# A first difference of weight blocks as a negated ScalarE copy and an accumulating transfer inside SBUF

## The chip, the core and the metric

The kernel runs on one core of a Trainium2 chip. The engines named here are TensorE (PE in the profile; PEld is its weight load), VectorE (DVE), ScalarE (ACT), GpSimd (POOL) and SyncE (SP). Transfers are issued by SP, ACT or POOL and carried by the core's 16 DMA engines. SBUF is the on-chip memory of 128 partitions, PSUM the accumulator memory behind TensorE, in eight banks of 512 float32 per partition. The metric is the device time of one execution in microseconds; all times below are microseconds unless marked ns.

## The reference

One decoder block on 256 tokens of width 2048: a gated convolution and a sparse attention side by side, an output mix, a layer norm, a feed-forward part and a second layer norm. The change is in the feed-forward part:

```python
x = _layer_norm(DN_ALPHA * x + mixed @ w_mix_out[i], ln1_g[i], ln1_b[i])
h = jnp.square(jax.nn.relu(x @ w_mlp_up[i])) @ w_mlp_down[i]
ple = (p[i] @ w_ple[i]) * jax.nn.sigmoid(x @ w_ple_gate[i])
x = _layer_norm(DN_ALPHA * x + h + ple, ln2_g[i], ln2_b[i])
```

`w_mlp_up` is 2048 x 8192, `w_mlp_down` 8192 x 2048, all in float32.

## The kernel before

**Splitting.** Every float32 operand is split in two: ScalarE rounds it to a high part (`hi`, type fp32r), VectorE subtracts that from the original to get the low part (`lo`). A product is then three matmuls: high by high, low by high, high by low. `split` (lines 67 to 70) does this for values and forms, `wchunk` (77 to 89) for a loaded piece of weights: one load to `raw` (four buffers) on SP's queue, `whi` on ScalarE (four buffers, line 86), `wlo` on VectorE (three buffers, line 88), each 128 x 1024 elements.

**The feed-forward loop.** It goes over four blocks `c` of 2048 hidden columns (line 1063). In a block, eight *pairs* `p` compute 256 hidden columns each: `up` (1035) runs `wstat` (91) in four steps of one weight piece, 8 wide matmuls (512 columns, line 106) and 8 narrow ones (256 columns, line 112) per step, then evacuates PSUM to `ab` (1041), adds, applies relu and square (1043 to 1045), splits the result into `h` (1046) and forms sums of its quarter blocks (`sums_to`, 629 to 637). `down` (1051) then multiplies the block's `h` by columns of `w_mlp_down` with `xstat` (131; matmuls at 144, 145, 148).

**Seven products.** The first two of the four column groups of `down` are not computed by `xstat`. For each pair the class `Seven` (639) treats a 2 x 2 arrangement of blocks of `h` and of a 256 x 1024 piece of `w_mlp_down` by seven block products in place of eight. The piece is loaded by `load` (648) as one 1 MB transfer to tile `rs` for even pairs and to the second half of tile `tr` for odd ones. In it `r[:, k, a]` is row block `k`, column half `a`. `b_forms` (653) splits two of its blocks as they are. `t_sums` (657) makes four differences and `t_forms` (664) splits them:

```python
nc.vector.tensor_sub(t13, r[:, :, 512:], r[:, 0, :].rearrange("p (a n) -> p a n", a=2))
nc.vector.tensor_sub(t24[:, 0], r[:, 1, 512:], t13[:, 0])
nc.vector.tensor_sub(t24[:, 1], t24[:, 0], r[:, 1, :512])
```

`t13` and `t24` are the first half of `tr` (two blocks of 512 each) and are used again by every pair. `products` (668) issues the seven products, three matmuls each (line 678), into seven PSUM banks that stay open for the whole block. In blocks 0 to 2 all eight pairs go this way, in block 3 the first four, 28 pieces in all; `second` (681) adds one more column block. Forms of pair `p` are made while pair `p + 1` runs its four steps `i` (`prep`, 1077 and 1090), its products 1 and 3 at step 0 of pair `p + 2`, the other five at step 2 (1085). After the last pair, steps of the third column of `down` take their place (1095 to 1111), and ten sums on the open banks follow (1105). Gates and the output mix use `Seven` too, through `side` (702), with the methods `t_sums` and `t_forms`.

**What sets the order.** The code lists work in program order, and a scheduler that models the engines then fixes one order for each engine, TensorE's interleaving of the blocks above included. On the chip each engine runs its list strictly in that order, and an instruction that waits holds up all behind it on the same engine. `after(x)` keeps an instruction behind `x`. SP's queue carries all weight loads, POOL's a few loads of constants and of the last weights (`rawl`, 1156; `gb_load`, 963).

Of the kernel before, what the change touches and what calls it, by code (L numbers as in the profile page):

```python
# [12 lines left out]
AF = mybir.ActivationFunctionType  # L13
ALU = mybir.AluOpType
# [31 lines left out]
def block_kernel(ctx: ExitStack, tc: tile.TileContext, x, p, w_in, conv_w, cmp_pe_k, cmp_w1_k, cmp_w2_k,  # L46
                 cmp_pe_v, cmp_w1_v, cmp_w2_v, w_conv_out, w_attn_out, w_mix_out, ln1_g, ln1_b,
                 w_mlp_up, w_mlp_down, w_ple, w_ple_gate, ln2_g, ln2_b, rel_bias, onehot, rowmask, out):
    nc = tc.nc
    x, p, w_in, conv_w, w_conv_out, w_attn_out, w_mix_out, w_mlp_up, w_mlp_down, w_ple, w_ple_gate, out = (  # L50
        a[0] for a in (x, p, w_in, conv_w, w_conv_out, w_attn_out, w_mix_out, w_mlp_up, w_mlp_down, w_ple,
                       w_ple_gate, out))
    p = p[0]
# [10 lines left out]
    def after(ins):  # L64
        return tc.issue_after(ins) if ins is not None else nullcontext()

    def split(src, hi, lo):
        last_hi[0] = nc.scalar.activation(hi, src, AF.Copy).ins  # L68
        last_lo[0] = nc.vector.tensor_sub(lo, src, f32(hi)).ins  # L69
        return last_lo[0]  # L70
# [102 lines left out]
    def bank(i):  # L173

        return psum.tile([P, 512], F32, tag=f"b{(2, 3, 0, 1, 4, 5, 6, 7)[i]}", name="s")

    def run(*gens):
        for g in gens:
            for _ in g:
                pass  # L180
# [5 lines left out]
    def weave(main, places, side):  # L186

        done = 0
        for at, _ in enumerate(main):
            while done < len(places) and places[done] <= at:  # L190
                next(side, None)
                done += 1
        run(side)
# [47 lines left out]
    def back(a, first, *dims):  # L241
        return bass.AP(tensor=a.tensor, offset=a.offset + first, ap=[list(a.ap[0])] + [list(d) for d in dims])
# [396 lines left out]
    class Seven:  # L639
# [13 lines left out]
        def b_forms(self, p):  # L653
            b = self.forms[:, self.b(p):self.b(p) + 4]
            split(back(self.raws[p], 0, (1536, 2), (1, 512)), b[:, 0:2], b[:, 2:4])

        def t_sums(self, p):
            r = self.raws[p]
            t13, t24 = self.ts[p] = self.t(p)
# [3 lines that stand above are left out]
# [31 lines left out]
    def in_pairs(w):  # L694
        return w.rearrange("(q k p) n -> p q k n", k=2, p=P)
# [263 lines left out]
    def gb_load(dst, i, v):  # L959

        with after(last_wlo[0]):
            nc.vector.memset(dst[:, i, 0:1], 0.0)
        nc.gpsimd.dma_start(dst[:, i, :], v.to_broadcast([P, D]))
# [71 lines left out]
    def up(c, p, banks):  # L1035

        ps = [b.rearrange("p (a t) -> p a t", a=2) for b in banks]
        yield from wstat(w_mlp_up, c * 2048 + p * 256, x1, None, ps=ps)
        ab = post.tile([P, 2, 2, T], F32, tag="m2", name="ab", bufs=2)
        for f in range(2):  # L1040
            nc.scalar.activation(ab[:, f], ps[f], AF.Copy)  # L1041
        m = ab[:, :, 0, :]
        nc.vector.tensor_add(m, m, ab[:, :, 1, :])
        nc.scalar.activation(m, m, AF.Relu)
        nc.scalar.activation(m, m, AF.Square)
        split(m, h[:, 2 * p:2 * p + 2, 0, :], h[:, 2 * p:2 * p + 2, 1, :])
        if p < sv.n:
            sv.sums[p] = post.tile([P, 4, 2, P], F32R, tag="sg", name="sums")
            sums_to(m, sv.sums[p])

    def down(c, j, banks):
        cs = slice(j * 512, (j + 1) * 512)

        def ev(t, ps):
            nc.vector.tensor_add(y[:, t, cs], y[:, t, cs], ps)
            if c == 3:
                nc.vector.bn_stats(stats2[:, t, j, :], y[:, t, cs])

        k0 = sv.n * 2 % KT if j < 2 else 0
        return xstat(w_mlp_down, j * 512, 512, h, ev, r0=c * 2048 + k0 * P, nkt=KT - k0, ps=banks, kt0=k0), ev  # L1060


    for c in range(4):
        h = big.tile([P, KT, 2, T], F32R, tag="B", name="h")
        forms = post.tile([P, 16, 512], F32R, tag="C", name="forms", bufs=1)
        tr = big.tile([P, 8, 512], F32, tag="O", name="tr")
        tf = tr[:, 0:4]

        def raw(p):
            if p % 2 == 0:  # L1070
                return late.tile([P, 2, 1024], F32, tag="rs", name="rs", bufs=1)
            return tr[:, 4:8].rearrange("p (k a) n -> p k (a n)", k=2)

        sv = Seven(in_pairs(w_mlp_down[c * 2048:(c + 1) * 2048]), 0, h, raw, lambda p: (tf[:, 0:2], tf[:, 2:4]), forms,
                   lambda p: 8 + p % 2 * 4, 0, n=8 if c < 3 else 4)
        acc = sv.acc
        prep = (sv.b_forms, sv.t_sums, sv.t_forms)
        (y00, y01), (y10, y11) = [[y[:, t, a:a + 512] for a in (0, 512)] for t in range(2)]
        u2, u3, u4 = tf[:, 0], tf[:, 1], tf[:, 2]
        if c == 3:  # L1080
            break
        for p in range(8):
            pair = up(c, p, [bank(6), bank(7)] if p == 1 else [bank(0), bank(1)])
            for i in range(4):
                if p >= 2 and i in (0, 2):
                    sv.products(p - 2, (5, 7, 6, 4) if i else (1, 3))
                next(pair)
                if i == 2:
                    sv.load(p)
                if p >= 1 and i < 3:  # L1090
                    prep[i](p - 1)
            run(pair)
        sv.products(6, (1, 3, 5, 7, 6, 4))
        third = down(c, 2, [bank(0), bank(1)])[0]
        for i in range(8):
            next(third)
            if i < 3:
                prep[i](7)
            if i == 3:
                sv.products(7, (1, 3))  # L1100
            if i == 4:
                sv.products(7, (5, 7, 6, 4))
            if i == 5:
                nc.scalar.activation(u2, acc[1], AF.Copy)
                for out_, a, b, op in ((y00, y00, acc[1], ALU.add), (y01, y01, acc[3], ALU.add),
                                       (u2, u2, acc[6], ALU.add), (u4, u2, acc[5], ALU.add),
                                       (u3, u2, acc[7], ALU.add), (y11, y11, acc[5], ALU.add),
                                       (y10, y10, acc[4], ALU.subtract), (y01, y01, u4, ALU.add),
                                       (y10, y10, u3, ALU.add), (y11, y11, u3, ALU.add)):
                    with after(last_wlo[0]):  # L1110
                        nc.vector.tensor_tensor(out_, a, b, op=op)
        run(third)
        ps = bank(4)
        weave(down(c, 3, [bank(2), bank(3)])[0], (1, 3, 5, 6), sv.second(ps))
        nc.vector.tensor_add(y[:, 0, 0:512], y[:, 0, 0:512], ps)
# [3 lines left out]
    for p in range(8):  # L1119
        pair = up(3, p, [bank(6), bank(7)] if p == 1 else [bank(0), bank(1)])  # L1120
        for i in range(4):
            if 2 <= p < 6 and i in (0, 2):
                sv.products(p - 2, (5, 7, 6, 4) if i else (1, 3))
            if p >= 6 and i == 0:
                next(p2)
            next(pair)
            if p < 4 and i == 2:
                sv.load(p)
            if 1 <= p < 5 and i < 3:
                prep[i](p - 1)  # L1130
            if p == 5 and i == 0:
                nc.scalar.activation(u2, acc[1], AF.Copy)
            if p == 5 and i == 3:
                for out_, a, b, op in ((u2, u2, acc[6], ALU.add), (y01, y01, acc[3], ALU.add), (u4, u2, acc[5], ALU.add),
                                       (u3, u2, acc[7], ALU.add), (y11, y11, acc[5], ALU.add),
                                       (y10, y10, acc[4], ALU.subtract), (y01, y01, u4, ALU.add),
                                       (y10, y10, u3, ALU.add), (y11, y11, u3, ALU.add)):
                    with after(last_wlo[0]):
                        nc.vector.tensor_tensor(out_, a, b, op=op)
            if p == 7 and i == 0:  # L1140
                with after(last_wlo[0]):
                    nc.vector.tensor_add(y00, y00, acc[1])
        run(pair)
        if p == 6:
            gb2 = big.tile([P, 2, D], F32, tag="O", name="gb2")
            gb_load(gb2, 0, ln2_g)
# [90 lines left out]
```

## Time and profile before

| what | time |
|---|---|
| median of 3 runs | 1798.98 (1798.4 to 1799.77) |
| span of the profiled execution | 1797.8, which is 1.2 under that median |
| TensorE busy | 1789.0 |
| VectorE busy | 1394.0 |
| ScalarE busy | 1005.9 |
| POOL busy | 18.4 |
| the stage of the four feed-forward blocks | from 1101 on |

The profile is one execution, recorded instruction by instruction. A row of a group tells how many instructions it has, what they wrote and read with shapes, and their durations in ns as minimum, median and maximum, or as busy time and mean. A row of a timeline or of the chain tells start, length, engine, line, operation and count; in square brackets stands how long the engine was idle before and what ended that. A row of waits tells who waited for whom: total, times, longest. A row of transfers tells destination, source, the issuing queue, count, size and the median time from issue to landing. A row of a stretch tells start and end, its length, the busy time and count of PE, PEld, DVE, ACT and POOL, the granted clock, the busy share of the DMA engines and GB/s. Matmuls overlap in the pipeline, so their pace is read from the chain (one after another), not from the length of one.

### The profile page before, as it was taken

Reading aid. Unit: us, or ns where it says so; the run is one execution under the profiler, and the core shown is the slowest. Engines: PE = TensorE matmul, PEld = TensorE weight load, DVE = VectorE, ACT = ScalarE, POOL = GpSimd, SP = SyncE. Lnnn points to the kernel's source line nnn. Section 1 sums busy time; section 2 is a strip of 40 time slices with the busy share of each in tenths; the row PEclk is TensorE's granted clock in tenths of the full one; section 3 lists DMA queues with packets and bytes.
Section 4 is the critical chain, followed back from the end, with each engine's and each line's share of the span. In section 5 each row is a group of like instructions: output and inputs, shape, how many; then the busy total and the mean of one; then the engine's idle time right before and its main releaser. Section 6 shows DMA issues by size and latency. Waiting matters only on the chain.

```text
span 1797.8 us, 24999 instructions
## 1 busy us (share of the span) xinstructions
PE 1789.0 (100%) x9277; PEld 1532.2 (85%) x9277; DVE 1394.0 (78%) x2064; ACT 1005.9 (56%) x1366; POOL 18.4 (1%) x33
## 2 busy tenths in 40 slices
PE   9999999999999999999999999999999999999998
PEld 7889888888888888888888888888888888888886
DVE  6776776777787997897798768886798689768765
ACT  5555555555555555555454745764576376637661
POOL 1000000000000000000000000000000000000010
PEclk9999999999999999999999999999999999999999
DMA  8777665566656665865685577754865586567672
GB/s 260 225 240 202 189 180 165 164 176 177 178 161 187 216 206 188 278 202 181 188 283 167 186 242 239 230 188 160 275 220 165 177 278 208 165 210 233 193 280 71
DMA packets 255849, 365.50 MB, mean 203 GB/s; under 512 B 10821, under 2 KB 175525, under 8 KB 255216
## 3 DMA queue, kind: packets, MB, share of 16 engines
q1 hardware_dynamic: 250944, 352.49, 62.1%
q0 software_dynamic: 2112, 8.81, 1.4%
q10 hardware_dynamic: 2672, 2.62, 0.5%
q8 instruction: 72, 1.18, 0.3%
q14 instruction: 49, 0.40, 0.1%
HBM read 361.76 MB, written 2.12 MB: 202 GB/s over the span
## 4 chain that ended last, share of the span: by engine, by line
PE 99%; DVE 0%; DMA 0%; ACT 0%; issue 0%; SPq 0%; DVEq 0%
PE mm L106 16%; PE s L106 13%; PE s L144 11%; PE s L145 11%; PE s L148 11%; PE s L678 11%; PE mm L112 9%; PE s L112 7%; PE s L688 2%; PE s L1169 1%; PE sc L500 1%; PE mm L144 1%; PE mm L145 1%; PE mm L148 1%; PE po L350 1%; PE po L572 1%
## 5 line engine op out<-in xcount | busy, mean ns | idle before, releaser
L86 ACT ACTIVATE whi<-raw 128x1024 fp32r<-128x1024 f32 (+2 forms) x576 | 598.9, 1043 | 504.9 <-PE s L145 213.4
L88 DVE TENSOR_TENSOR wlo<-raw,whi 128x1024 fp32r<-128x1024 f32 (+2 forms) x576 | 688.0, 1202 | 232.7 <-PE s L148 75.8
L106 PE MATMUL mm<-xT,whi 128*128 128x512 f32 x1280 | 313.6, 393 | 0.1
L106 PEld LDWEIGHTS mm<-xT,whi 128*128 128x128 f32 x1280 | 234.0, 189 | 44.9 <-issue 0.6
L106 PE MATMUL s<-x,whi 128*128 128x512 f32 x1024 | 263.1, 391 | 0.0
L106 PEld LDWEIGHTS s<-x,whi 128*128 128x128 f32 x1024 | 184.3, 188 | 32.3
L112 PE MATMUL mm<-xT,wlo 128*128 128x256 f32 x1280 | 181.5, 285 | 0.0
L112 PEld LDWEIGHTS mm<-xT,wlo 128*128 128x128 f32 x1280 | 170.0, 190 | 7.5
L112 PEld LDWEIGHTS s<-x,wlo 128*128 128x128 f32 x1024 | 141.9, 190 | 11.6
L112 PE MATMUL s<-x,wlo 128*128 128x256 f32 x1024 | 145.2, 282 | 0.0
L69 DVE TENSOR_TENSOR forms<-tr,forms 128x1024 fp32r<-128x1024 f32 x82 | 98.6, 1222 | 16.6 <-ACT forms L68 16.6
L145 PE MATMUL s<-whi,h 128*128 128x512 f32 x256 | 99.6, 389 | 0.0
L68 ACT ACTIVATE forms<-tr 128x1024 fp32r<-128x1024 f32 x82 | 84.9, 1051 | 25.9 <-PE s L678 9.2
L144 PE MATMUL s<-whi,h 128*128 128x512 f32 x256 | 99.3, 389 | 0.0
L678 PE MATMUL s<-forms,sums 128*128 128x512 f32 x336 | 85.1, 390 | 0.0
L148 PE MATMUL s<-wlo,h 128*128 128x512 f32 x256 | 79.4, 389 | 0.0
L678 PEld LDWEIGHTS s<-forms,sums 128*128 128x128 f32 x336 | 62.6, 188 | 12.9
L1041 ACT ACTIVATE ab<-s 128x512 f32<-128x512 f32 x64 | 37.4, 593 | 47.1 <-PE s L106 47.1
L678 PE MATMUL s<-forms 128*128 128x512 f32 x240 | 60.8, 389 | 0.0
L148 PEld LDWEIGHTS s<-wlo,h 128*128 128x128 f32 x256 | 48.1, 188 | 10.0
L144 PEld LDWEIGHTS s<-whi,h 128*128 128x128 f32 x256 | 48.1, 188 | 9.9
L145 PEld LDWEIGHTS s<-whi,h 128*128 128x128 f32 x256 | 48.1, 188 | 9.9
(336 smaller groups left out, 2753.1 us busy)
## 6 DMA issues: line engine op xcount, KB each, us to landing
raw<-in_w_in_dram SPq DMA_DIRECT2D x204, 512.0 KB, 4.3
raw<-in_w_mlp_up_dram SPq DMA_DIRECT2D x128, 512.0 KB, 4.7
raw<-in_w_mlp_down_dram SPq DMA_DIRECT2D x78, 512.0 KB, 4.2
raw<-in_w_conv_out_dram SPq DMA_DIRECT2D x32, 512.0 KB, 4.5
raw<-in_w_attn_out_dram SPq DMA_DIRECT2D x32, 512.0 KB, 4.3
raw<-in_w_ple_gate_dram SPq DMA_DIRECT2D x32, 512.0 KB, 4.1
rs<-in_w_mlp_down_dram SPq DMA_DIRECT2D x14, 1024.0 KB, 7.3
tr<-in_w_mlp_down_dram SPq DMA_DIRECT2D x14, 1024.0 KB, 7.0
```

Of the source, the lines that this page charges most:

```text
L68: last_hi[0] = nc.scalar.activation(hi, src, AF.Copy).ins
L69: last_lo[0] = nc.vector.tensor_sub(lo, src, f32(hi)).ins
L86: last_whi[0] = nc.scalar.activation(hi, raw, AF.Copy).ins
L88: last_wlo[0] = nc.vector.tensor_sub(lo, raw, f32(hi)).ins
L106: last_mm[0] = nc.tensor.matmul(ps[f].rearrange("p a t -> p (a t)"), hi[:, kk, f * P:(f + 1) * P], mov[:, k0 + kk].rearrange("p a t -> p ( ...
L112: last_mm[0] = nc.tensor.matmul(ps[f][:, 1, :], lo[:, kk, f * P:(f + 1) * P], mov[:, k0 + kk, 0, :], start=False, stop=False, skip_group_c ...
L144: nc.tensor.matmul(ps[t], sta[:, kt0 + kt, 0, ts], hi[:, kk, :], start=(kt == 0), stop=False)
L145: nc.tensor.matmul(ps[t], sta[:, kt0 + kt, 1, ts], hi[:, kk, :], start=False, stop=False)
L148: last_mm[0] = nc.tensor.matmul(ps[t], sta[:, kt0 + kt, 0, ts], lo[:, kk, :], start=False, stop=(kt == nkt - 1)).ins
L678: last_mm[0] = nc.tensor.matmul(self.acc[n], first[:, a, :], self.forms[:, w, :], start=(p == 0 and i == 0), stop=(p == self.n - 1 and i = ...
L688: last_mm[0] = nc.tensor.matmul(ps, self.mat[:, 2 * (q + k) + 1, a, 0:P], w[:, k, :], start=(own is not None and q + k == 0 and i == 0), s ...
L1041: nc.scalar.activation(ab[:, f], ps[f], AF.Copy)
```

## The change

`t13`, the first difference, is no longer VectorE's. ScalarE writes the negated first row block to `t13`, and POOL issues a transfer from SBUF to SBUF that adds the right halves of both row blocks (512 KB) to it in flight. The rest of the old `t_sums` stays on VectorE as `t_second`. Only the feed-forward loop uses the new methods; gates and mix keep `t_sums`. The four parts of `prep` now take four steps: copy and transfer together with `b_forms` at step 0, nothing at step 1, the other two differences at step 2, `t_forms` at step 3, where it was 0, 1, 2. At the end of a block the last products and the sums move one step back.

```diff
+        def t_first(self, p):
+            r = self.raws[p]
+            t13, _ = self.ts[p] = self.t(p)
+            nc.scalar.activation(t13, r[:, 0, :].rearrange("p (a n) -> p a n", a=2), AF.Copy, scale=-1.0)
+            nc.gpsimd.dma_start(t13, r[:, :, 512:], accum_op=ALU.add)
+
+        def t_second(self, p):
+            r, (t13, t24) = self.raws[p], self.ts[p]
+            nc.vector.tensor_sub(t24[:, 0], r[:, 1, 512:], t13[:, 0])
+            nc.vector.tensor_sub(t24[:, 1], t24[:, 0], r[:, 1, :512])
...
-        prep = (sv.b_forms, sv.t_sums, sv.t_forms)
+        prep = (lambda p: (sv.t_first(p), sv.b_forms(p)), lambda p: None, sv.t_second, sv.t_forms)
...
-                if p >= 1 and i < 3:
+                if p >= 1:
                     prep[i](p - 1)
...
-            if i < 3:
+            if i < 4:
                 prep[i](7)
-            if i == 3:
+            if i == 4:
                 sv.products(7, (1, 3))
-            if i == 4:
+            if i == 5:
                 sv.products(7, (5, 7, 6, 4))
-            if i == 5:
+            if i == 6:
                 nc.scalar.activation(u2, acc[1], AF.Copy)
...
-            if 1 <= p < 5 and i < 3:
+            if 1 <= p < 5:
                 prep[i](p - 1)
```

In the changed file everything below line 656 stands 11 lines lower: the copy is L660, the transfer L661, the two differences L665 and L666; relu, square and the addition of `ab` are L1055, L1056 and L1054.

The scheduler makes a new order of it. VectorE at the first pair of block 0 (`wlo` are weight splits, `ple_gb` and `y` belong to the stage before, `forms` are split forms), before:

```order
L660 TENSOR_TENSOR tr<-rs 128x1024
L88 TENSOR_TENSOR wlo<-raw,whi 128x1024
L661 TENSOR_TENSOR tr<-rs,tr 128x512
L662 TENSOR_TENSOR tr<-tr,rs 128x512
L88 TENSOR_TENSOR wlo<-raw,whi 128x1024
L995 TENSOR_TENSOR ple_gb<-sg,ple_gb 128x512 x2
L955 SCALAR_TENSOR_TENSOR y<-y,ple_gb 128x512 x2
```

and now:

```order
L665 TENSOR_TENSOR tr<-rs,tr 128x512
L1006 TENSOR_TENSOR ple_gb<-sg,ple_gb 128x512 x2
L666 TENSOR_TENSOR tr<-tr,rs 128x512
L966 SCALAR_TENSOR_TENSOR y<-y,ple_gb 128x512
L88 TENSOR_TENSOR wlo<-raw,whi 128x1024
L966 SCALAR_TENSOR_TENSOR y<-y,ple_gb 128x512
L88 TENSOR_TENSOR wlo<-raw,whi 128x1024
L69 TENSOR_TENSOR forms<-rs,forms 128x1024
L88 TENSOR_TENSOR wlo<-raw,whi 128x1024
L69 TENSOR_TENSOR forms<-tr,forms 128x1024 x3
```

The subtraction that needed only the load is gone; the one that needs the transfer (L665) now stands ahead of the split weights and forms.

VectorE at the second pair of blocks 1 to 3, from its first row on the piece's second difference to the split of `sums`, before:

```order
L661 TENSOR_TENSOR tr<-tr 128x512
L1043 TENSOR_TENSOR ab<-ab 128x2x256
L88 TENSOR_TENSOR wlo<-raw,whi 128x1024
L662 TENSOR_TENSOR tr<-tr 128x512
L88 TENSOR_TENSOR wlo<-raw,whi 128x1024
L633 TENSOR_TENSOR sa<-ab 128x128
L635 TENSOR_TENSOR sa<-ab 128x128
L69 TENSOR_TENSOR h<-ab,h 128x2x256
```

and now:

```order
L665 TENSOR_TENSOR tr<-tr 128x512
L633 TENSOR_TENSOR sa<-ab 128x128
L635 TENSOR_TENSOR sa<-ab 128x128
L666 TENSOR_TENSOR tr<-tr 128x512
L634 TENSOR_TENSOR sa<-sa,ab 128x128
L69 TENSOR_TENSOR h<-ab,h 128x2x256
L88 TENSOR_TENSOR wlo<-raw,whi 128x1024
L636 TENSOR_TENSOR sa<-ab,sa 128x128
L88 TENSOR_TENSOR wlo<-raw,whi 128x1024
L69 TENSOR_TENSOR sums<-sa,sums 128x4x128
```

The addition of `ab` and two weight splits now stand ahead of L665, and `h` and `sums` behind it.

ScalarE in a later pair of a block (`h` its high part, `forms` the high parts of forms), before:

```order
L1044 ACTIVATE ab<-ab 128x2x256
L68 ACTIVATE forms<-tr 128x1024 x2
L1045 ACTIVATE ab<-ab 128x2x256
L86 ACTIVATE whi<-raw 128x1024
L68 ACTIVATE h<-ab 128x2x256
L86 ACTIVATE whi<-raw 128x1024 x2
```

and now:

```order
L1055 ACTIVATE ab<-ab 128x2x256
L68 ACTIVATE forms<-tr 128x1024
L1056 ACTIVATE ab<-ab 128x2x256
L68 ACTIVATE h<-ab 128x2x256
L660 ACTIVATE tr<-tr 128x1024
L86 ACTIVATE whi<-raw 128x1024
```

The negated copy (L660) has come in behind the high part of `h`; POOL's transfer waits for it, and on VectorE the next L665 for the transfer.

## The prediction

> **What bounds the kernel now.** I read the page's busy times first, then the chain that ended last, then the waits of TensorE, and then looked for a plain measure of how full TensorE is.
>
> ```profile
> PE 1789.0 (100%) x9277; PEld 1532.2 (85%) x9277; DVE 1394.0 (78%) x2064; ACT 1005.9 (56%) x1366; POOL 18.4 (1%) x33
> PE 99%; DVE 0%; DMA 0%; ACT 0%; issue 0%; SPq 0%; DVEq 0%
> PE po L287 <- DVE tab L301: 1.5, 1, 1.5
> PE sc L223 <- DMA xnat<-in_x_dram: 0.7, 1, 0.7
> PE s L1022 <- ACT row L1018: 0.4, 1, 0.4
> PE mm L144 <- ACT whi L86: 0.3, 1, 0.3
> PE tp L223 <- DMA xnat<-in_x_dram: 0.2, 1, 0.2
> ```
>
> TensorE is busy all the time, 99% of the chain lies on it, and its whole list of waits comes to 3.1 us, at the start (lines 223, 287, 144) and at the very end (1022); none lies in the feed-forward blocks that the change touches. Whether "busy" hides slow matmuls there is told by the chain in order of time:
>
> ```profile
> 28.76 3.65 PE mm L106 x16
> 34.32 3.65 PE mm L106 x16
> 1138.82 3.65 PE s L678 x16
> 1154.07 3.65 PE s L678 x16
> 1275.90 5.47 PE s L106 x24
> 1446.87 5.47 PE s L106 x24
> ```
>
> Sixteen wide matmuls (512 columns) take 3.65, so one takes 0.228; between 28.76 and 34.32 come sixteen wide and sixteen narrow ones (256 columns), so a narrow one takes (5.56 - 3.65)/16 = 0.12. One feed-forward block holds 616 wide and 256 narrow ones: 616 x 0.2275 + 256 x 0.12 = 170.9. The two rows at 1275.90 and 1446.87 are the same point of blocks 1 and 2, 170.97 apart. So TensorE has no gap there at all, and one pair of a block takes 15.25 (1138.82 to 1154.07). Time saved on VectorE can't shorten this; the change can only leave TensorE fed, or starve it.
>
> **What the change removes and adds.** Per pair it takes one 128x1024 subtraction from VectorE and gives ScalarE a copy of the same size, 28 times.
>
> ```profile
> L660 DVE TENSOR_TENSOR tr<-rs x14: 1217/1220/1227, 1099.3 to 1655.8; 128x1024 f32<-128x1024 f32 x14
> L661 DVE TENSOR_TENSOR tr<-rs,tr x14: 684/686/691, 1101.6 to 1658.7; 128x512 f32<-128x512 f32 x14
> L68 ACT ACTIVATE forms<-tr 128x1024 fp32r<-128x1024 f32 x82 | 84.9, 1051 | 25.9 <-PE s L678 9.2
> 1315.25:1330.50 15.25, 15.25 (x86) 13.31 (x86) 14.98 (x24) 10.81 (x16) 0.00 (x0) 1.00 0.72 229
> ```
>
> VectorE loses 28 x 1.22 = 34 us, ScalarE gains 28 x 1.05 = 29 us. The last row is one pair by stretches (PE, PEld, DVE, ACT, POOL busy): VectorE 14.98 of 15.25, ScalarE 10.81. Both fit, VectorE better than before; worth on the end: 0, since TensorE covers both. What is new is the transfer between them: the second difference now waits for copy, POOL's issue and landing. Call the time from issue to landing L. No row shows an accumulating transfer, nor one from SBUF to SBUF. The nearest:
>
> ```profile
> rawl<-in_w_mlp_down_dram POOLq DMA_DIRECT2D x8, 512.0 KB, 4.7
> raw<-in_w_mlp_down_dram SPq DMA_DIRECT2D x78, 512.0 KB, 4.2
> gb<-in_ln_g_dram POOLq DMA_DIRECT2D x1, 1024.0 KB, 7.5
> out_dram<-y SPq DMA_DIRECT2D x6, 256.0 KB, 2.1
> DMA to landing us min/median/max: 4.8/7.0/9.4
> 1282.00:1297.00 15.00, 15.00 (x91) 13.30 (x90) 13.44 (x18) 10.93 (x14) 0.00 (x0) 1.00 0.91 307
> ```
>
> `rawl` has the very shape (128 rows of 2 x 512) and the same queue: 4.7. Low end: out of SBUF 256 KB took 2.1; a second 256 KB at 307/0.91 = 337 GB/s adds 0.8, POOL instead of SP adds 4.7 - 4.2 = 0.5: 3.4. High end: the addition reads source and destination, 1 MB, and POOL's 1 MB load took 7.5; among the 1 MB loads of tile rs (the row of minimum, median and maximum) the slowest took 9.4. Between 3.4 and 9.4 I take **L = 6.5**, nearer to the 1 MB rows, because two operands are read.
>
> [...]
>
> **Where a late landing reaches TensorE.** VectorE works in a fixed order, so whatever stands behind the waiting subtraction (L665 in the changed file) waits too: weight splits, `sums` and `h` that TensorE needs. The first two pairs of each block are tight:
>
> ```profile
> 1092.18 0.50 SPq L651 DMA_DIRECT2D rs<-in_w_mlp_down_dram  x1
> 1099.30 1.23 DVE L660 TENSOR_TENSOR tr<-rs 128x1024 f32<-128x1024 f32 x1 [2.12 <-DMA rs<-in_w_mlp_down_dram]
> 1101.13 1.98 PE L106 MATMUL s<-x,whi 128*128 128x512 f32 x8
> 1270.36 1.13 PE s L106 x5
> 1273.73 1.06 ACT L68 ACTIVATE forms<-rs 128x1024 fp32r<-128x1024 f32 x1 [2.50 <-DMA rs<-in_w_mlp_down_dram]
> 1350.03 0.29 DVE L636 TENSOR_TENSOR sa<-ab,sa 128x128 f32<-128x128 f32 x1
> ```
>
> *Block 0, first pair.* The 1 MB load lands at 1099.30 (VectorE waited for it). Now ScalarE's copy starts there: 1099.30 + 1.05 = 1100.35, and L665 can start at 1100.35 + L. From its start to the end of the next weight split VectorE has L665, L1006 twice, L666 and L966, 0.69 each, and the split, 1.22: 4.67. TensorE wants that split after 28 wide and 24 narrow matmuls of the new block, 1101.13 + 9.25 = 1110.4. So L may be 1110.4 - 4.67 - 1100.35 = 5.4.
>
> *Block 0, second pair.* Its copy must wait until the first pair's difference is split (in the new order six operations of 0.69 and five of 1.22 from L665 on: 10.2). L665 of the second pair starts at 1100.35 + L + 10.2 + 1.05 + L = 1111.6 + 2L. From it to the end of `sums` stand four operations of 0.69, four of 0.29 and two of 1.22: 6.4. TensorE wants `sums` after 77 wide and 80 narrow matmuls, 1101.13 + 27.1 = 1128.2. So TensorE waits 1111.6 + 2L + 6.4 - 1128.2 = 2L - 10.2 by then, the first pair's wait included.
>
> *Blocks 1 to 3.* The load lands at 1273.73 in block 1, and the same arithmetic with 5.0 (0.69, 1.22, 0.69, 1.22, 1.22) between the two pairs gives L665 at 1273.73 + 1.05 + L + 5.0 + 1.05 + L = 1280.8 + 2L; `sums` is wanted after 84 wide and 79 narrow matmuls from 1270.36, at 1298.9; wait 2L - 11.7 each.
>
> With L = 6.5: 2.8 + 3 x 1.3 = **6.7 us**. With L = 3.4: nothing. With 9.4: 8.6 + 3 x 7.1 = 30.
>
> *Weight loads beside it.* In the first pairs the DMA engines are 0.91 busy (the stretch 1282 to 1297). Reading 1 MB more at 337 GB/s is 3.1 of 16-engine time: 13.65 + 3.1 = 16.8 in a stretch of 15, so loads there land up to 1.75 later, and one of them is waited for already:
>
> ```profile
> 1282.62 1.06 ACT L86 ACTIVATE whi<-raw 128x1024 fp32r<-128x1024 f32 x1 [3.50 <-DMA raw<-in_w_mlp_up_dram]
> ```
>
> Four blocks, 0 to 1.75 each, 0 to 7; I take half, **3.5 us**.
>
> *Later pairs.* There a ring closes: L665 0.69, weight split 1.22, L666 0.69, the addition of `ab` 0.69 on VectorE; relu 0.62, a form 1.05, square 0.63, the high part of `h` 0.63 and the next copy 1.05 on ScalarE:
>
> ```profile
> 1343.83 0.62 ACT L1044 ACTIVATE ab<-ab 128x512 f32<-128x512 f32 x1
> 1344.48 0.63 ACT L1045 ACTIVATE ab<-ab 128x512 f32<-128x512 f32 x1
> 1345.15 0.63 ACT L68 ACTIVATE h<-ab 128x512 fp32r<-128x512 f32 x1
> ```
>
> 3.29 + 3.98 = 7.27, plus L. It fits into 15.25 while L is under 8.0, so with 6.5 these pairs cost 0. At the end of a block the last products and the sums on them stand one step later (i of 4, 5, 6 for 3, 4, 5). The next column of `down` overwrites the banks of products 1 and 3; their readers, a copy of 0.6 and two additions of 0.69, still have the last step, 12 wide matmuls or 2.7, so 0, but 2.0 of 2.7 is close. SP's reload of the raw buffer stands behind L666, as it stood behind the old third subtraction; later by at most L665's wait, which is in the sums above. POOL has nothing else queued until the last block's `rawl` and `gb`, issued after the last of the 28.
>
> Sum: 1797.8 + 6.7 + 3.5 = 1808.0 for the span. The profiled execution's span is 1.2 under the median of the runs (1798.98), so **1809**.
>
> **Rivals.**
> *A, forecast (0.42): the first pairs of the blocks starve TensorE,* L from about 5.8 to 8.5: 1.4 to 23 in the sum above, plus 0 to 7: 1803 (under that it is no change) to 1829. Its own range is 1803 to 1820. For it: the 1 MB rows, and VectorE's fixed order.
> *B, hidden (0.36).* The transfer lands in under 5.5 or so, as a 512 KB one does on this queue (4.7) and as data leaving SBUF does (2.1 for 256 KB); VectorE's 1.22 less per pair absorbs the rest. Then 1798 to 1802, about 1799. [...] Against it: DMA share 0.91 just there.
> *C, the ring (0.18).* The addition in the transfer is slow (two passes, or L over 9). Then each later pair is as long as the ring: 7.27 + L instead of 15.25. It decides from L = 8.0; with 9.5 it costs 1.5 x about 13 pairs, 20, on top of 31 in the first pairs: 1853; with 12 some 1900. For it: nothing shows the operation's price; against it: the slowest 1 MB load, itself in a crowd, took 9.4.
> *D, faster (0.04).* VectorE's 34 us buy TensorE time. At most the 3.1 us of waits, 1796, and those lie elsewhere; a small gain would be noise.
>
> **How the numbers follow.** About 0.2% (3.6 us) can be told from no change. Slower: A and C, 0.60; same: B, 0.36; faster: D, 0.04. The likeliest case gives 1809. The range reaches down into B, to 1797.5, and up to where C has begun, L near 9 (7.8 + 3 x 6.3 + 13 + 3.5 is 43): 1845; beyond it I leave about a tenth.
>
> **What would show it.** POOL's 28 transfers, from issue to landing: 5.8 to 8.5 for A. VectorE's idle time before L665, ended by the transfer, in nearly every pair, longest in the first two of each block. TensorE waits in the first pairs of the blocks, for VectorE's `wlo` and `sums` products, and none later; equal points of blocks 1 and 2 then stand some 172 to 175 apart and not 170.97. If TensorE's list of waits stays at 3 us, B was right; if later pairs are longer than 15.25, C. Wrong altogether would be waits for weight loads (`raw`) in the middle of blocks, or a matmul pitch other than 0.228.

## The result and the profile after

The changed kernel takes **1816.55 us** (median of 4 runs, 1815.56 to 1818.08) beside 1799.38 (1798.4 to 1799.86) for the kernel before: ratio 1.0094, 95% interval 1.0082 to 1.0106, or 17.2 us more. Forecast were 1809 and a range of 1797.5 to 1845, "slower" with 0.60. The direction and the place were right; the cost was 10.2 in the sum and 17.2 on the chip. The profiled execution after has a span of 1816.0, 18.2 longer than the one before (1797.8).

The page of the changed kernel (busy times, the chain that ended last, POOL's DMA queue with packets, MB and share of 16 engines, and two groups of DMA issues with the median time to landing):

```profile
PE 1794.9 (99%) x9277; PEld 1533.9 (84%) x9277; DVE 1363.0 (75%) x2036; ACT 1030.4 (57%) x1394; POOL 51.8 (3%) x61
PE 87%; DMA 7%; issue 3%; DVE 2%; ACT 1%; SPq 0%; DVEq 0%; POOLq 0%
q0 software_dynamic: 9728, 23.49, 6.9%
raw<-in_w_mlp_up_dram SPq DMA_DIRECT2D x128, 512.0 KB, 6.1
```

VectorE lost 31 us of work and ScalarE gained 25, about as reckoned. But the chain, which lay to 99% on TensorE, now has 7% on transfers. TensorE's list of waits (total, times, longest) has two new lines in the feed-forward blocks:

```profile
PE s L112 <- DVE wlo L88: 11.2, 7, 4.7
PE s L689 <- DVE h L69: 0.8, 2, 0.6
```

The transfer itself (L661, duration on POOL in ns and the time from issue to landing as minimum, median and maximum), and then what VectorE's first use of it (L665) waited for:

```profile
L661 POOL DMA_DIRECT2D tr<-rs x14: 1176/1185/1254, 1100.3 to 1669.4; - x14
DMA to landing us min/median/max: 6.1/6.4/10.8
```

```profile
  DMA tr<-rs: 39.5, 11
  DMA tr<-tr: 10.2, 11
```

The median landing L is 6.4 (6.5 was taken), but the slowest takes 10.8, and VectorE stands still for it 49.7 us in 22 of 28 pairs. How that reaches TensorE is seen in block 1, in the chain that ended last (start, length, what), then in VectorE's and TensorE's timelines:

```profile
1268.81 7.37 DMA rs<-in_w_mlp_down_dram
1276.21 1.07 ACT tr L660
1277.57 9.48 DMA tr<-rs
1287.08 1.07 ACT forms L68
```

```profile
1279.39 2.35 DVE L88 TENSOR_TENSOR wlo<-raw,whi 128x1024 fp32r<-128x1024 f32 x2
1287.08 0.69 DVE L665 TENSOR_TENSOR tr<-rs,tr 128x512 f32<-128x512 f32 x1 [5.33 <-DMA tr<-rs]
1289.91 1.22 DVE L88 TENSOR_TENSOR wlo<-raw,whi 128x1024 fp32r<-128x1024 f32 x1
```

```profile
1291.19 1.21 PE L112 MATMUL s<-x,wlo 128*128 128x256 f32 x8 [2.50 <-DVE wlo L88]
1292.24 3.82 PE L106 MATMUL s<-x,whi 128*128 128x512 f32 x16
1466.10 3.82 PE L106 MATMUL s<-x,whi 128*128 128x512 f32 x16
```

The 1 MB load, the copy and the transfer follow one another; the transfer lands 9.48 after its issue; L665 waits 5.33; the weight split behind it ends at 1291.1, and TensorE, out of weights, has stood for 2.50. The two rows of sixteen wide matmuls are the same point of blocks 1 and 2, now 173.86 apart and not 170.97.

Laying TensorE's rows against its gapless pitch (0.228 and 0.12 per matmul) gives how far it falls behind in each block: 2.9, 4.2, 3.2 and 8.8, 19.1 together, all of it behind the transfers of a block's first three pairs.

### The profile page after: what moved, and what is told of

It reads as the page before. It is cut to its first block, busy times and chain, and to the rows that moved or that the text cites. A ratio compares the mean times of both kernels' runs of the same rounds, so it can differ in the third digit from the quotient of the medians.

```text
span 1816.0 us, 25127 instructions
## 1 busy us (share of the span) xinstructions
PE 1794.9 (99%) x9277; PEld 1533.9 (84%) x9277; DVE 1363.0 (75%) x2036; ACT 1030.4 (57%) x1394; POOL 51.8 (3%) x61
## 3 DMA queue, kind: packets, MB, share of 16 engines
q0 software_dynamic: 9728, 23.49, 6.9%
## 4 chain that ended last, share of the span: by engine, by line
PE 87%; DMA 7%; issue 3%; DVE 2%; ACT 1%; SPq 0%; DVEq 0%; POOLq 0%
PE mm L106 16%; PE s L144 11%; PE s L145 10%; PE s L148 10%; PE s L689 9%; PE mm L112 8%; PE s L106 8%; PE s L112 4%; DMA rs<-in_w_mlp_down_dram 3%; DMA tr<-rs 3%; PE s L699 1%; PE s L1180 1%; PE sc L500 1%; PE mm L144 1%; DVE wlo L88 1%
## 5 line engine op out<-in xcount | busy, mean ns | idle before, releaser
L112 PEld LDWEIGHTS s<-x,wlo 128*128 128x128 f32 x1024 | 141.0, 191 | 23.4 <-DVE wlo L88 12.8
L112 PE MATMUL s<-x,wlo 128*128 128x256 f32 x1024 | 145.7, 283 | 11.2 <-DVE wlo L88 11.2
L689 PEld LDWEIGHTS s<-forms 128*128 128x128 f32 x240 | 45.0, 188 | 9.3
```

What stands on the lines that cost most here:

```text
L112: last_mm[0] = nc.tensor.matmul(ps[f][:, 1, :], lo[:, kk, f * P:(f + 1) * P], mov[:, k0 + kk, 0, :], start=False, stop=False, skip_group_c ...
L689: last_mm[0] = nc.tensor.matmul(self.acc[n], first[:, a, :], self.forms[:, w, :], start=(p == 0 and i == 0), stop=(p == self.n - 1 and i = ...
```

## The experiments

The ratio is against runs of the kernel before taken beside it. The last column says what the run had in common with which kernel: the scheduler orders all instructions anew for each program, so a variant can differ from the changed kernel in more than its edit. I compared the order of each engine's instructions, line numbers aside.

| run | median | ratio and interval | instruction order |
|---|---|---|---|
| `e1_moved`, new steps, no transfer | 1800.73 | 1.0008 (0.9999 to 1.0017) | nearly that of before |
| `e9_load`, transfers that nobody reads, no copies | 1801.18 | 1.0007 (0.9998 to 1.0016) | nearly that of before |
| `e4_plain`, transfer without the addition | 1800.12 | 1.0001 (0.9991 to 1.0011) | exactly that of the changed kernel |
| `e7_half`, half of it by transfer | 1799.63 | 0.9996 (0.9987 to 1.0006) | its own |
| `e6_twice`, two transfers in series | 1933.84 | one execution | its own |
| `e3_first`, pairs 0 to 2 of a block only | 1818.16 | 1.0106 (1.0083 to 1.0129) | its own |
| `e2_later`, all but pairs 0 to 2 | 1803.30 | 1.0019 (1.0009 to 1.0029) | its own |
| `e12_only0`, pair 0 of a block only | 1813.17 | 1.0070 (1.0055 to 1.0086) | its own |
| `e11_from1`, all but pair 0 | 1820.64 | 1.0111 (1.0088 to 1.0134) | its own |
| `e13_early`, raw load of pair 1 earlier | 1821.02 | 1.0111 (1.0096 to 1.0126) | nearly that of the changed kernel |
| `e5_unread`, unread copies and transfers | 1811.84 | 1.0071 (1.0056 to 1.0086) | its own |
| `e8_copy`, unread copies alone | 1810.49 | 1.0054 (1.0038 to 1.0071) | its own |

One of the four executions of `e8_copy` took 6381; it is in the median but not in the ratio.

### The moved steps alone

```diff
-            nc.scalar.activation(t13, r[:, 0, :].rearrange("p (a n) -> p a n", a=2), AF.Copy, scale=-1.0)
-            nc.gpsimd.dma_start(t13, r[:, :, 512:], accum_op=ALU.add)
+            nc.vector.tensor_sub(t13, r[:, :, 512:], r[:, 0, :].rearrange("p (a n) -> p a n", a=2))
```

> The changed order of steps is kept (four steps of preparation, products and sums one step later), but VectorE makes the first difference again and there is no transfer. Theory A (the wait for the transfer in the first pairs costs the time): 1797 to 1802, no change from the kernel before. Rival (the later products and sums at the end of a block cost it, the step I put at 0): 1806 or more, and TensorE waits stand at the block ends.

1800.73, not to be told from no change. The later products and sums at the block ends cost nothing that can be measured, as the prediction had it.

### The load alone

A tile of 448 columns twice (`gap`, set to zero once) takes the results, and VectorE makes the difference as before. These lines take the place of the copy and of the transfer to `t13`.

```diff
+            nc.gpsimd.dma_start(gap, r[:, :, 512:960], accum_op=ALU.add)
+            nc.vector.tensor_sub(t13, r[:, :, 512:], r[:, 0, :].rearrange("p (a n) -> p a n", a=2))
```

> As the kernel with the unread transfers, but without the copies: 28 accumulating transfers of 448 KB into a place that nothing reads (they add onto what is there), issued when the raw load has landed, with nobody waiting for them. Theory T (load on the DMA engines): 1807 to 1812. Rival S (ScalarE's copy): 1799 to 1804.

1801.18: the 28 transfers with nobody waiting cost 0 to 2.9 us, and no change is inside the interval. Theory T falls; so does the 3.5 us that the prediction put on later weight loads. It is not that these transfers were quick:

```profile
DMA to landing us min/median/max: 5.0/6.4/11.0
```

Over all 28 they land about as late as in the changed kernel, if not at the same places (see the crowd below). What nobody waits for costs nothing here.

### The addition alone

```diff
-            nc.gpsimd.dma_start(t13, r[:, :, 512:], accum_op=ALU.add)
+            nc.gpsimd.dma_start(t13, r[:, :, 512:])
```

> The changed kernel with a plain transfer in place of the accumulating one; the first difference isn't computed (the transfer overwrites the negated copy), all waits are the same. Theory R (the addition reads two operands, which makes both the landing time and the load): issue to landing 4.4 to 5.0 against 6.4, time 1801 to 1808. Rival Q (queue, descriptors and the crowd set the landing, the addition is free): 6.0 or more, time 1813 to 1818.

1800.12 against 1800.32 for the kernel before: the whole loss is gone. Every engine has the same instructions in the same order as in the changed kernel, with ScalarE's copy, the wait and the queue all there; only the addition in the transfer is missing. So this pair of kernels (1.0094 and 1.0001, each against runs of the kernel before beside it) is the cleanest comparison of the study. The view of L661 (time to landing), then POOL's queue on the page, then VectorE in block 1:

```profile
DMA to landing us min/median/max: 3.2/3.8/6.9
```

```profile
q0 software_dynamic: 6144, 23.49, 4.0%
```

```profile
1277.02 2.35 DVE L88 TENSOR_TENSOR wlo<-raw,whi 128x1024 fp32r<-128x1024 f32 x2
1279.45 0.69 DVE L665 TENSOR_TENSOR tr<-rs,tr 128x512 f32<-128x512 f32 x1
```

L665 starts without a wait where the changed kernel waited 5.33. The landing is 3.8 and not 6.4, and theory R holds over theory Q, though both landing and time lie under what was expected of it (4.4 to 5.0, and 1801 to 1808). The queue shows what the addition does. The kernel before has, for what else runs on this queue:

```profile
q0 software_dynamic: 2112, 8.81, 1.4%
```

(6144 - 2112)/28 = 144 packets for a plain transfer, (9728 - 2112)/28 = 272 for an accumulating one, for the same bytes written. In time of all 16 engines it is (4.0% x 1797.8 - 1.4% x 1797.8)/28 = 1.7 and (6.9% x 1816.0 - 1.4% x 1797.8)/28 = 3.6 us. How the extra packets divide into reads and writes no view here shows.

### Half the size

The copy and the transfer make one half of `t13`, VectorE the other.

```diff
+            nc.scalar.activation(t13[:, 0], r[:, 0, :512], AF.Copy, scale=-1.0)
+            nc.gpsimd.dma_start(t13[:, 0], r[:, 0, 512:], accum_op=ALU.add)
+            nc.vector.tensor_sub(t13[:, 1], r[:, 1, 512:], r[:, 0, 512:])
```

> Only one of the two 128x512 differences goes by ScalarE and the accumulating transfer (256 KB), VectorE makes the other before it waits. Theory A (the wait decides, and it falls with the bytes: plain 512 KB 3.8, with the addition 6.4, so the second read is worth 2.6 and 256 KB with the addition reads as much as 512 KB plain): issue to landing about 3.8, at most 5.5 at the block starts, time 1799 to 1803. Rival F (a transfer of this kind has a large fixed part): landing 5.5 or more, time 1807 to 1813.

1799.63, theory A. The landings of the 28 accumulating transfers of 256 KB:

```profile
DMA to landing us min/median/max: 3.3/4.4/5.6
```

So a smaller wait on the same place costs nothing that can be measured (ratio 0.9996). It takes work off VectorE and is no slower than the kernel before, nor is it faster: TensorE has no gap to fill. No run beats the kernel before.

### Twice the wait

```diff
             nc.gpsimd.dma_start(t13, r[:, :, 512:], accum_op=ALU.add)
+            nc.gpsimd.dma_start(t13, r[:, :, 512:], accum_op=ALU.add)
```

> Each accumulating transfer is issued twice in series on the same place (the right half is then added twice, so another result is computed). If the second starts when the first has landed, issue to landing is about 12.8 in all. The ring of the later pairs is then 7.27 + 12.8 = 20.1 against a pair of 15.25: with 13 pairs that is 63, and the first pairs cost 2 x 12.8 - 10.2 + 3 x (2 x 12.8 - 11.7) = 57; about 1930, range 1900 to 1950. If the later pairs don't close a ring (they have more slack than I reckoned): 1850 to 1880, with the loss in the first pairs alone.

1933.84 in one execution, beside 1930 expected. The expectation's own terms, 63 and 57, add to 120, which is about 1919 and not 1930. They were to be waits, but TensorE's waits in these blocks add to 91. From 1095 to 1800 the mean granted clock is 0.94, which is some 85 us at 0.50 and so up to 42 us of slower matmuls, a term that the arithmetic doesn't have. So the nearness of the number is in good part luck, and what the run shows is the ring. It can be read from POOL's timeline of this kernel, where the first transfer of each pair starts four times at

```profile
1574.90 1.19 POOL L661 DMA_DIRECT2D tr<-rs  x1 [11.47 <-ACT tr L660]
1595.45 1.19 POOL L661 DMA_DIRECT2D tr<-tr  x1 [12.96 <-ACT tr L660]
1614.76 1.19 POOL L661 DMA_DIRECT2D tr<-rs  x1 [11.07 <-ACT tr L660]
1635.28 1.19 POOL L661 DMA_DIRECT2D tr<-tr  x1 [11.85 <-ACT tr L660]
1655.97 1.19 POOL L661 DMA_DIRECT2D tr<-rs  x1 [11.19 <-ACT tr L660]
```

(1655.97 - 1574.90)/4 = 20.3 per pair, against 7.27 + 12.8 = 20.1. The same ring stands in the changed kernel, where the transfers chase a TensorE that needs 15.25 per pair:

```profile
1501.90 1.19 POOL L661 DMA_DIRECT2D tr<-tr  x1 [10.90 <-ACT tr L660]
1515.67 1.19 POOL L661 DMA_DIRECT2D tr<-rs  x1 [12.58 <-ACT tr L660]
1529.49 1.19 POOL L661 DMA_DIRECT2D tr<-tr  x1 [12.63 <-ACT tr L660]
1543.44 1.19 POOL L661 DMA_DIRECT2D tr<-rs  x1 [12.75 <-ACT tr L660]
```

(1543.44 - 1501.90)/3 = 13.8, against 7.27 + 6.4 = 13.7. VectorE and the transfer gain 1.4 on TensorE in each later pair, until the lag of the first pairs is made up; that is why these pairs cost nothing.

### Which pairs

Four variants choose the pairs by one line ahead of the copy; the others take VectorE's difference and return.

```diff
+            if p < 3:          # e2_later;  e3_first: p > 2;  e11_from1: p == 0;  e12_only0: p > 0
+                nc.vector.tensor_sub(t13, r[:, :, 512:], r[:, 0, :].rearrange("p (a n) -> p a n", a=2))
+                return
```

> The first three pairs of each block go back to VectorE's difference; the transfer is used in the 16 later pairs only (5 in each of three blocks, 1 in the last). Theory A: 1798 to 1801, since the ring of 7.27 + 6.4 = 13.7 fits into a pair's 15.25. Rival C' (each transfer costs TensorE something, by load on the DMA engines or by the ring): 16/28 of 17.2, about 1809.

> The converse: the transfer in the first three pairs of each block only (12 of 28), VectorE's difference in the later ones. Theory A: nearly all of the 17.2 is lost, 1812 to 1817. Rival C' (each transfer costs the same): 12/28 of 17.2, about 1807.

`e3_first` loses all of it (18.4 us) with 12 of 28 transfers, `e2_later` 3.5 with the other 16. So it is a matter of place and not of number. `e2_later` is a small miss for theory A too: TensorE waits 1.1 once, in block 2, behind the third transfer after the change-over, which lands in 9.7, and 0.7 in all at the ends of two blocks.

> The converse: the transfer in the first pair of each block only (4 of 28). The places where TensorE fell behind in the changed kernel's first pairs add to 1.3 + 2.7 + 1.4 + 5.7 = 11.1: about 1810 if the first weight split behind the wait is a bound of its own. By the sums alone, the only bound that I set for blocks 1 to 3, the second pair's L665 would start at 1281.0 + L against 1292.5, so nothing up to L = 11.5: 1800 to 1802, block 0's 1.4 included.

1813.17: the first pair alone costs 13.6, more than the 11.1 that the changed kernel's places add to. TensorE waits for the weight split 2.45 in block 1 and 2.48 in block 3, so this split is a bound of its own there (block 2 shows 0.6 on `sums` and no stop on the split). The prediction had that bound for block 0 only; for the others it used the sums of the second pair. Behind both stops the granted clock is 0.50 for 3.4, worth up to 3.4 in all, which neither expectation has.

> Only the first pair of each block goes back to VectorE's difference (4 of 28); all other pairs keep the transfer. Theory A1 (the first pair's transfer lands in the crowd at the block start, and the lag of the second and third pair is its consequence): 1799 to 1804. Rival A3 (each of the first three pairs costs its own part): 10 to 13 of 17 remain, 1809 to 1813.

1820.64, a miss for both theories. Without the first pair's transfer the loss isn't smaller. In block 1 of this kernel, the one transfer issued at 1288.84 on POOL's queue (landing), VectorE (L668 is the first use here) and TensorE:

```profile
tr<-tr POOLq DMA_DIRECT2D x1, 512.0 KB, 10.6
```

```profile
1299.49 0.69 DVE L668 TENSOR_TENSOR tr<-tr 128x512 f32<-128x512 f32 x1 [4.95 <-DMA tr<-tr]
```

```profile
1302.50 0.50 PE L112 MATMUL s<-x,wlo 128*128 128x256 f32 x2 [3.34 <-DVE wlo L88]
```

Now pair 1's transfer is the late one: 10.6, and 9.4 and 11.3 in blocks 2 and 3, where it took 6.8 to 7.1 in the changed kernel. So the long landing doesn't belong to the first pair, and theory A1 falls. Three stretches of 3.4 at a granted clock of 0.50 add up to 5.1 to this run's time.

### The crowd at the block start

The prediction had the DMA engines 0.91 busy there. With the first transfers of blocks 1 to 3 beside the loads they are full; in the changed kernel, the three stretches from issue to landing (PE, PEld, DVE, ACT and POOL busy, granted clock, DMA share, GB/s):

```profile
1277.50:1287.00 9.50, 9.50 (x55) 8.28 (x54) 4.12 (x4) 3.77 (x4) 1.19 (x1) 1.00 1.01 287
1452.60:1461.00 8.40, 8.40 (x49) 7.36 (x49) 4.28 (x5) 3.83 (x5) 1.19 (x1) 1.00 0.99 264
1627.80:1638.60 10.80, 10.26 (x57) 8.70 (x55) 3.50 (x3) 3.64 (x4) 1.19 (x1) 1.00 0.97 260
```

Full engines alone don't make a landing late: the second transfers of these blocks run at shares of 1.01 to 1.02 too and land in 6.8 to 7.1. Beside the transfer of block 1 runs the raw load of the second pair, 1 MB, issued 1.0 later. `e13_early` issues it ahead, right behind the first pair's (that is three steps of `prep` earlier; the expectation's "some five" was a miscount); the same edit stands in the loop of block 3.

```diff
-                if i == 2:
+                if i == 2 and p != 1:
                     sv.load(p)
+                if i == 3 and p == 0:
+                    sv.load(1)
```

> The changed kernel, but the second pair's 1 MB raw load is issued some five steps earlier (right behind the first pair's), so that it doesn't run beside the first transfer of the block. Theory W (the crowd of that load makes the first transfer 8 to 11): the first transfers of blocks 1 to 3 land in 6 to 7, the sum of the two landings is about 13, time 1803 to 1808. Rival V (the loads of weights alone fill the DMA engines): they stay at 8 to 11, time 1812 to 1820.

1821.02, which is 1 above the range of rival V. The first transfers of blocks 1 to 3 land in 9.1, 9.2 and 9.5, as V had it. But the edit didn't take the 1 MB load out of their way. In block 1 it is issued (SP's timeline) 7.7 ahead of the transfer, takes 10.9 to land, and so runs beside it for another 3.2; in blocks 2 and 3 it is 3.3 and 3.5. Then the DMA issues of block 1 in a window from the transfer's issue to its landing:

```profile
1269.45 0.81 SPq L651 DMA_DIRECT2D tr<-in_w_mlp_down_dram  x1
```

```profile
raw<-in_w_mlp_up_dram SPq DMA_DIRECT2D x3, 512.0 KB, 9.9
tr<-rs POOLq DMA_DIRECT2D x1, 512.0 KB, 9.1
```

So the run doesn't decide between W and V. The second transfers land late here as well (11.0, 9.4 and 10.3, where the changed kernel has 6.8 to 7.1), with the next 1 MB load issued 0.5 to 0.8 behind them.

The traces of the changed kernel and of `e3_first`, `e11_from1`, `e12_only0` and `e13_early` together say more. Sorted by how long after the transfer's issue the next 1 MB raw load is issued, the transfers land as follows:

| 1 MB load issued after the transfer by | transfers | issue to landing |
|---|---|---|
| 0.1 to 1.0 | 12 | 9.3 to 11.3 |
| 1.1 to 1.2 | 3 | 7.2 to 8.4 |
| 1.6 to 2.5 | 13 | 6.3 to 7.1, and one of 8.4 |

All others land in 6.0 to 7.2, but for the first ones of `e13_early` (8.8 to 9.5), beside which a 1 MB load is in flight for another 3.2 to 3.9. In `e9_load`, where the load follows 4.8 behind the first transfers of blocks 1 to 3, these (448 KB) land in 5.8 each; its slowest, 11.0, has the load 0.5 behind it. So the late landings go with a 1 MB load issued within about 1 us, whichever pair it is. That this load is the cause isn't shown, since no run moves it alone; nor is why a microsecond matters.

### The copies and the transfers that nothing reads

These lines take the place of the copy and of the transfer to `t13`; `gap` is the tile of above.

```diff
+            nc.scalar.activation(gap, r[:, 0, :].rearrange("p (a n) -> p a n", a=2)[:, :, :448], AF.Copy, scale=-1.0)
+            nc.gpsimd.dma_start(gap, r[:, :, 512:960], accum_op=ALU.add)      # e8_copy: without this line
+            nc.vector.tensor_sub(t13, r[:, :, 512:], r[:, 0, :].rearrange("p (a n) -> p a n", a=2))
```

> All 28 copies and accumulating transfers run (7/8 of their size, for want of room), into a place that nothing reads, and VectorE makes the difference itself: the load on ScalarE and on the DMA engines without the wait. Theory A (the wait itself): 1798 to 1803, of which the load makes up to 3.5. Rival (the load on the DMA engines delays the weight loads, and that is most of the loss): 1808 to 1816, with TensorE waiting for weight products whose loads landed late.

> As the kernel with the unread transfers (VectorE makes the difference, +12 us there), but without the transfers: only the 28 copies on ScalarE, into a place that nothing reads. Theory T (the transfers load the DMA engines and make the loads of the first pairs late): 1799 to 1803. Rival S (the copy waits in ScalarE's fixed order for the 1 MB raw load and holds up the high parts of weights and of h behind it): 1806 to 1812.

1811.84 and 1810.49. By the number alone `e5_unread` speaks for the rival, load on the DMA engines. But `e8_copy` has no transfer at all and loses nearly as much, and `e9_load` has all of the load and loses nothing. What the copy (L660) waited for in `e8_copy`, and then in the changed kernel:

```profile
  DMA rs<-in_w_mlp_down_dram: 38.5, 14
  DMA tr<-in_w_mlp_down_dram: 17.9, 10
```

```profile
  DMA rs<-in_w_mlp_down_dram: 9.1, 4
```

With no reader, the scheduler put the copy so early that ScalarE, which works in its fixed order, stood 56.4 us for raw loads, in 24 of 28 pairs, with the steps of `ab` and the sums behind it. In the changed kernel it is 9.1 in 4. So these two runs made a new wait of their own; they show what a copy at the wrong place costs (10 us), and nothing on the changed kernel.

## Why the prediction was right, and where it was off

- **TensorE bounds, VectorE's 34 us buy nothing:** right. `e4_plain` has VectorE relieved by the same amount and takes 1800.12 beside 1800.32.
- **L from issue to landing, 6.5 between 3.4 and 9.4:** the median is 6.4. The 1 MB that it was reckoned from, two operands of 512 KB, was my estimate, as was the 3.1 us of DMA time that rests on it; no view tells reads from writes. What the runs show is the price of the addition: 6.4, 272 packets and 3.6 us of all 16 DMA engines with it, 3.8, 144 and 1.7 without it (`e4_plain`).
- **L as one number for all pairs:** this is the step that failed, a term mis-sized. The first landings of the four blocks, in the changed kernel's DMA issues by window:

```profile
tr<-rs POOLq DMA_DIRECT2D x1, 512.0 KB, 6.8
tr<-rs POOLq DMA_DIRECT2D x1, 512.0 KB, 9.5
tr<-rs POOLq DMA_DIRECT2D x1, 512.0 KB, 8.3
tr<-rs POOLq DMA_DIRECT2D x1, 512.0 KB, 10.8
```

The second ones are 6.3, 6.8, 7.1 and 6.8. The formulas were 2L - 10.2 for block 0 and 2L - 11.7 for the others; with the two landings of each block in place of 2L they give 2.9, 4.6, 3.7 and 5.9, together **17.1** where the prediction had 6.7. Measured were 2.9, 4.2, 3.2 and 8.8. That blocks 1 and 2 come out so near is in part luck: by the end of the second pair, where the formula counts, TensorE had fallen behind by 3.6 and 2.6, and the third pair, which the prediction puts at nothing, added 0.8 in each. The prediction had quoted the share of 0.91 and the slowest 1 MB load of 9.4, but used them for a term of its own and for the range, not for the first landings.
- **Block 3, 2.9 above the formula:** the clock. TensorE's timeline there, and then its stretches:

```profile
1636.95 1.11 PE L112 MATMUL s<-x,wlo 128*128 128x256 f32 x8
1642.74 2.08 PE L112 MATMUL s<-x,wlo 128*128 128x256 f32 x8 [4.69 <-DVE wlo L88]
1644.62 5.70 PE L106 MATMUL s<-x,whi 128*128 128x512 f32 x16
```

```profile
1642.00:1645.00 3.00, 2.25 (x9) 2.21 (x10) 3.00 (x4) 3.00 (x5) 1.12 (x1) 0.50 0.30 70
1645.00:1648.00 3.00, 3.00 (x8) 2.31 (x7) 3.00 (x5) 2.97 (x6) 0.08 (x1) 0.50 1.08 238
```

After the stop of 4.69 the granted clock is 0.50: eight narrow matmuls take 2.08 and not 1.11, sixteen wide ones 5.70 and not the 3.82 that the timeline has for them behind the stop of 2.50 in block 1: 2.9 in all. The prediction had no such term.
- **Weight loads later, 3.5:** 0 as far as can be measured: `e9_load`, whose transfers go out at other moments, loses 0 to 2.9, and the changed kernel's list of TensorE waits has no new line on a weight load. They did land later (6.1 and not the 4.7 of the page before). Two errors, this and the one on L, partly cancelled.
- **The bound in blocks 1 to 3:** TensorE waited mainly for the weight split behind the first L665 (11.2 of 12.0 us of new waits), and for the products on `h`, 0.8; `sums`, which I had named for these blocks, isn't in the list. With an L of 6.5 that first split would just have been in time (it would end at 1288.1, and TensorE wants it at 1288.7); at 9.5 it binds first.
- **Later pairs, 0 while 7.27 + L is under 15.25:** right from the fourth pair on, with 13.8 measured, and 20.3 with the wait doubled; the third pair cost 0.8 in blocks 1 and 2 and 1.0 in block 3.
- **Block ends, SP's order:** 0 was right (`e1_moved` and `e4_plain`).
- **What would show it:** the median landing, VectorE's waits, the waits for `wlo` and the 172 to 175 between equal points (173.86) all came. Waits before L665 are longest in the first and third pair of a block, not in the first two.

The rivals: B would have held with a landing of 3.8, as `e4_plain` shows, C from two transfers on, as `e6_twice` shows. Of the 19.1 that TensorE falls behind, its list of waits names 12.0 and the clock 2.9; about 4 lie in steps too small for a row, and I leave them unexplained.

## What to carry to other kernels

When work goes from a busy engine to a transfer, price the transfer where it will be issued and not by its median: here 8.3 to 10.8 for the first transfers of blocks 1 to 3, where a 1 MB load was issued within 1.2 behind them, and 6.1 to 7.1 elsewhere; blocks 1 to 3 lost 16 of the 19. Ask what stands in order behind the first reader of the result; 49.7 us of waiting on VectorE became 12 on TensorE only where the engine had no lead. And an experiment on a scheduled program must be read with its instruction order: of twelve variants only one kept the order of the kernel that it explains.

## What the runs showed of the hardware

- An accumulating SBUF transfer of 512 KB on POOL's queue: 6.4 from issue to landing (6.1 to 10.8), 1.19 of POOL's time, 272 packets, 3.6 us of all 16 DMA engines. A plain one: 3.8 (3.2 to 6.9), 144 packets, 1.7 us. An accumulating one of 256 KB: 4.4 (3.3 to 5.6). So the addition isn't free: in time of the DMA engines it costs about what a second plain transfer costs.
- Behind the stop of TensorE of 4.69 us came some 6 us at a granted clock of 0.50, behind one of 5.20 in `e13_early` too. The length of the stop alone doesn't decide: the clock stayed at 1.00 behind the 2.50 of the changed kernel and fell to 0.50 behind the 2.45 of `e12_only0`. What differs in the traces is how the stop lies against the changes of the clock. The stretch at 0.50 in block 3 of the changed kernel is 6.83 long (1641.78 to 1648.61), twice 3.41, and those of `e12_only0` are 3.4. Cut into stretches of 3.41 counted from those changes, the stop of 2.50 falls into two, the one of 2.45 into one. First the changed kernel, then `e12_only0` with the stretch behind it:

```profile
1286.80:1290.20 3.40, 1.89 (x13) 1.52 (x11) 2.72 (x4) 2.18 (x3) 0.00 (x0) 1.00 0.94 329
```

```profile
1287.70:1291.10 3.40, 0.95 (x8) 0.75 (x7) 3.40 (x4) 2.45 (x3) 0.00 (x0) 1.00 0.51 174
1291.20:1294.40 3.20, 3.20 (x11) 2.72 (x11) 3.20 (x4) 3.04 (x5) 0.00 (x0) 0.50 0.56 164
```

TensorE stood for 1.51 of the first (3.40 - 1.89) and for 2.45 of the second (3.40 - 0.95). In the feed-forward blocks of the changed kernel, cut this way, one stretch at full clock was followed by 0.50, the one from 1638.37 to 1641.78, in which TensorE stood throughout; in the others it stood for at most 1.52. That the clock goes by such stretches is my reading of these few changes; from how much standing on it falls, these runs don't show.
